# A hybrid decoder on one core: half-array products gathered into runs, and the first loads, the bias table and the first norm rearranged

## The chip, the cores and the metric

The kernel runs on 1 core of one Trainium2 chip. The metric is the device time of one execution in microseconds (us); the time before is the median of three runs. PE is TensorE, DVE is VectorE, ACT is ScalarE, POOL is GpSimd, SP is SyncE, which issues most of the transfers.

## The reference

Two layers of a decoder over 256 tokens of width 1024, all in float32. Each layer normalises `x`, projects it, runs three groups of heads, and adds the result to `x`; then a SwiGLU feed-forward part does the same.

```python
def reference(x, ...):
    for l in range(DEPTH):                       # 2
        h = rms_norm(x, attn_norm[l])
        proj = h @ w_in[l]
        r_q, r_k, r_v, r_g, n_q, n_kv, n_g, gm_z = jnp.split(proj, split_points, axis=-1)
        ret_o = retention(rope(r_q), rope(r_k), r_v, r_g)            # 6 heads of 64
        nsa_o = nsa(n_q, n_kv, n_g, ..., rel_bias)                   # 6 heads, 2 key groups
        gm_o = spatial_gating(gm_z, gm_ws[l], gm_b[l])
        x = x + jnp.concatenate([ret_o, nsa_o, gm_o], -1) @ w_out[l]
        h = rms_norm(x, ffn_norm[l])
        gate, up = jnp.split(h @ w_gate_up[l], 2, axis=-1)
        x = x + (jax.nn.silu(gate) * up) @ w_down[l]
    return x
```

Retention forms scores of queries and keys per head in chunks of 128 tokens, multiplies them by a decay and sums values with them. The sparse attention `nsa` adds a bias from a table of 32 buckets by 6 heads (`rel_bias`) that depends on the distance of query and key alone, so that each row of the bias is the row before, shifted by one.

## The kernel before

The weights, 109.86 MB in all with the other loads, stream from HBM in 102 pieces per layer (`PIECES`, L69 to L87). A piece goes into one of three staging buffers `wst`, ACT casts it to the matmul format (`whi`, six buffers), DVE subtracts the cast from the original (`wlo`, six buffers), and PE multiplies with both parts, so that each product is made of three: high by high, high by low, low by high. `stream_load`, `stream_hi` and `stream_lo` (L463 to L497) are these three steps. The normalised `x` is split in the same way into `hh` and `hl` (both in the tile `hcat`).

The projection `w_in` is cut into seven groups of columns, in the order `nk`, `nq`, `gm`, `nv`, `rq`, `rk`, `rg` (`ORDER`, L49): keys, queries, gated part, values of the sparse attention, then the four groups of retention. `nk` has 5 pieces, `nq` and `gm` 4, `nv` 3, the others 4. `project` (L1271) issues 48 products for a group: 8 slices of the inner dimension, 2 tiles of 128 tokens, 3 products. They write the PSUM banks `acc`; all else on PE writes the banks `sm`. Behind the groups come the output projection, the feed-forward part's first matrix in 11 chunks, and its second.

Nobody writes the order of instructions by hand. Each part of the work is a generator that yields operations; the class `Desk` (L259) holds a clock for each engine with cost estimates (`_cost_PE` and the like, L200) and picks at each step the waiting operation of best priority on the engine that is free first. A yielded list goes to its engine without a break. The order so found is fixed when the kernel is built; at run time an engine works its own queue in order and waits on semaphores.

What the change touches:

- `START` and `load_start` (L155, L558): the first transfers on SP. `x` comes in four quarters (two tiles of tokens, two halves of columns), "w" stands for the next piece of weights. The small table `par` (gains) stands between them. `norm_part` (L643) transposes a quarter with four products, scales it on ACT and subtracts on DVE; `norm_scale` (L676) works out the reciprocal root of one tile's mean square by some 15 operations of one column on DVE.
- `warm_up` (L546): products of zeros ("fillers", `sm<-w2k`) that PE is given while it has nothing else before the end of the first project.
- `load_layer` and `setup_bias` (L579, L600): the other small loads, and the bias. One product of the one-hot table `oh` with `relb` gives a row of 384 values for each of 6 heads on 6 partitions; a POOL transfer writes it 33 times to the DRAM tensor `scr`; four POOL transfers read it back, shifted by one for each partition, as `B` (128 partitions, 6 heads, 256 keys). POOL copies parts of it to `Bc`. `unit` (L1004) needs both for the scores of a head.
- `retention` (L1159): `scores(p)` (L1168) yields for a pair of heads a list of two products of 256 and one of two products of 128 columns, each over 64 rows of the array (`sm<-qkT`, 64*128 in the trace); then per head a list of six products of 64 columns onto half of the array's columns (`sm<-rv,S`, 128*64).
- `pv` (L1059): for each of three pairs of heads one product with `vbd` (96 rows, compressed part) and eight with `V` (`sm<-PT,V`, 128*64), which all add into one bank. `PT` holds the attention weights.

Of the kernel before, what the change touches and what calls it, by code (L numbers as in the profile page):

```python
# [9 lines left out]
F32 = mybir.dt.float32  # L10
F32R = mybir.dt.float32r
I32 = mybir.dt.int32
# [142 lines left out]
START = [(0, 0), "w", (1, 0), "w", "w", (0, 1), (1, 1), "w"]  # L155
# [28 lines left out]
class Engine:  # L184
# [5 lines left out]
    def __getattr__(self, method):  # L190
        fn = getattr(self.eng, method)

        def make(*a, prio=None, lat=True, **k):
            dur, table = getattr(self, "_cost_" + self.name)(method, a, k)
            banks = {x.tensor.name for x in (*a, *k.values()) if _psum(x)}
            return Op(self.name, lambda: fn(*a, **k), dur, table, lat, prio, banks)  # L196

        return make
# [60 lines left out]
class Desk:  # L259
# [4 lines left out]
    def __init__(self, preload):  # L264
        self.preload = preload
        self.free = {e: 0.0 for e in self.LAT}
        self.free["DMA"] = 1500.0
# [123 lines left out]
class Trunk:  # L391
    def __init__(self, ctx, tc, x, wts, cst, oh, relb, par, w1, w2, wsT, out):
# [17 lines left out]
        self.scale2 = [self.fixed(f"scale2{t}", [128, 1]) for t in range(2)]  # L410
# [15 lines left out]
        self.started = False  # L426

# [58 lines left out]
    def stream_lo(self):  # L486
        for i in range(L * len(PIECES)):
# [8 lines left out]
            self.desk.give(self.wst, self.st.pop(i))  # L496
# [23 lines left out]
    def setup(self):  # L520
# [16 lines left out]
        self.ev_cst, self.ev_bias = Event(), Event()  # L537
# [8 lines left out]
    def warm_up(self):  # L546
# [5 lines left out]
        while not self.started:  # L552
            n = 256 if self.desk.free["PE"] < Desk.COLD else 128
            yield self.PE.matmul(ps[:, :n], w[:, :128], w[:, :n], start=True, stop=True, lat=False, prio=2000)
# [3 lines left out]
    def load_start(self):  # L558

        SP, fire, lat = self.SP, self.desk.fire, self.desk.LAT["DMA"]  # L560
        yield SP.dma_start(self.ident, self.d["cst"][:, C_ID : C_ID + 128], lat=False)
        i = 0
        for step in START:
# [9 lines left out]
            if step == (0, 0):  # L573
                yield SP.dma_start(self.par, self.d["par"][0], lat=False)
                fire(self.ev_par[0], lat)
# [3 lines left out]
    def load_layer(self, l):  # L579
# [6 lines left out]
        yield SP.dma_start(self.wsT, self.d["wsT"][l].rearrange("p (g t) -> p g t", g=4))  # L586
        yield G.tensor_tensor(
            self.wsT, self.wsT, self.tri[:, None, :].to_broadcast([128, 4, 128]), op=ALU.mult
        )
# [6 lines left out]
        if l == 0:  # L596
            yield SP.dma_start(self.cst[:, C_DEC:], self.d["cst"][:, C_DEC:])
            self.desk.fire(self.ev_dec)

    def setup_bias(self):  # L600

        G, GQ, PE = self.G, self.GQ, self.PE
        oh = yield Need(self.w2k)
        ext = yield Need(self.w2k)
        rb = self.tiny("rb", [33, 6])
# [1010 lines left out]
```

## Time and profile before

| | |
|---|---|
| median of 3 runs | 645.78 us (645.46 to 646.02) |
| the profiled execution, own time | 646.46 us |
| its span, first to last instruction | 644.7 us |
| PE busy | 635.1 us |
| DVE, ACT, POOL busy | 452.9, 364.8, 11.0 us |
| mean granted clock of TensorE | 0.997 |

The profile follows one execution. The durations in it are of that execution, whose time is 1.76 us more than its span and 0.68 us above the median. Products are pipelined on PE: the length shown for one product reaches to its modelled end, so the pace is read from one row's start to the next row's start. All operations carry the line of one helper (L196), so rows are told apart by tile names: `out<-in`, buffer numbers left out. A name such as 128*64 behind MATMUL is the part of the array (rows*columns) that is used; `x16` counts passes, two for each float32 product. A bracket at the end of a row is the idle time ahead of it and what ended it. The granted clock is the share of TensorE's full clock.

### The profile page before, as it was taken

To read this page: it belongs to the slowest core of one execution; us is meant where nothing else is said; L and a number is where in the kernel's file an instruction comes from. 1 tells how busy PE (TensorE), PEld (TensorE's weight loads), DVE (VectorE), ACT (ScalarE), POOL (GpSimd) and SP (SyncE) were. 2 spreads that over 40 slices of the span, in tenths; PEclk is the share of its full clock that TensorE was granted. 3 is DMA by queue.
4 is the path that set the end of the run, shared out by engine and by line. 5 is a ranking of instruction groups with operands and counts; after the bars stand their busy time and mean duration, and the time that the engine had idled before them with its cause. 6 is when DMAs were issued, how large, how long until landed. Compare 5 with 4: busy or idle time off the path is not lost.

```text
span 644.7 us, 9955 instructions
## 1 busy us (share of the span) xinstructions
PE 635.1 (99%) x3628; PEld 533.6 (83%) x3628; DVE 452.9 (70%) x1046; ACT 364.8 (57%) x685; POOL 11.0 (2%) x28
## 2 busy tenths in 40 slices
PE   8979999999999999999999999999999999999998
PEld 7768887788888888888887888788888888888886
DVE  5867988488677677664388899865867677776441
ACT  7648963576456555543377795444755555545330
POOL 0120000000000000010000000000000000000000
PEclk9999999999999999999999999999999999999999
DMA  8885245157555565566546522534665556565631
GB/s 257 284 228 175 91 123 181 66 166 231 190 180 192 185 196 192 185 257 204 163 135 196 196 92 64 173 110 149 186 191 185 193 195 187 174 197 184 192 114 65
DMA packets 32816, 111.63 MB, mean 173 GB/s; under 512 B 4339, under 2 KB 4851, under 8 KB 32512
## 3 DMA queue, kind: packets, MB, share of 16 engines
q1 hardware_dynamic: 32256, 109.86, 52.4%
q0 software_dynamic: 512, 1.14, 0.9%
q8 instruction: 28, 0.46, 0.3%
q14 instruction: 20, 0.16, 0.1%
HBM read 109.64 MB, written 1.35 MB: 172 GB/s over the span
## 4 chain that ended last, share of the span: by engine, by line
PE 89%; DMA 5%; ACT 2%; DVE 2%; issue 1%; SPq 0%; ACTq 0%
PE acc L196 60%; PE sm L196 29%; DMA wst<-in_wts_dram 5%; ACT whi L196 1%; DVE wlo L196 1%; DMA x<-in_x_dram 1%; DVE x L196 0%; SPq L196 0%; ACT w2k L196 0%; ACT L402 0%; ACT L196 0%; DVE Kl L196 0%; ACT Kh L196 0%; ACT hcat L196 0%; ACT w1k L196 0%
## 5 line engine op out<-in xcount | busy, mean ns | idle before, releaser
L196 DVE TENSOR_TENSOR wlo<-wst,whi 128x1024 fp32r<-128x1024 f32 (+3 forms) x204 | 245.0, 1202 | 140.8 <-ACT whi L196 139.6
L196 ACT CAST whi<-wst 128x1024 fp32r<-128x1024 f32 (+3 forms) x204 | 209.2, 1028 | 195.0 <-issue 49.7
L196 PE MATMUL acc<-whi,hcat 128*128 128x512 f32 (+2 forms) x512 | 141.2, 381 | 0.0
L196 PEld LDWEIGHTS acc<-whi,hcat 128*128 128x128 f32 x512 | 91.6, 189 | 15.0 <-issue 0.7
L196 PE MATMUL acc<-hcat,whi 128*128 128x512 f32 x320 | 101.2, 396 | 0.0
L196 PE MATMUL sm<-hcat,whi 128*128 128x512 f32 x320 | 99.7, 392 | 0.0
L196 PE MATMUL acc<-wlo,hcat 128*128 128x512 f32 (+2 forms) x256 | 80.6, 381 | 0.0
L196 PEld LDWEIGHTS sm<-hcat,whi 128*128 128x128 f32 x320 | 60.0, 188 | 14.2
L196 PEld LDWEIGHTS acc<-hcat,wlo 128*128 128x128 f32 x320 | 58.8, 188 | 11.7
L196 PE MATMUL sm<-hcat,wlo 128*128 128x256 f32 x320 | 64.4, 282 | 0.0
L196 PE MATMUL acc<-hcat,wlo 128*128 128x256 f32 x320 | 64.1, 282 | 0.0
L196 PEld LDWEIGHTS acc<-wlo,hcat 128*128 128x128 f32 x256 | 46.8, 189 | 7.8 <-issue 0.3
L196 PEld LDWEIGHTS acc<-hcat,whi 128*128 128x128 f32 x320 | 50.9, 190 | 1.7
L196 PE MATMUL acc<-whi,ah 128*128 128x512 f32 (+1 forms) x176 | 50.0, 378 | 0.0
L196 PE MATMUL acc<-whi,al 128*128 128x512 f32 (+1 forms) x176 | 50.0, 378 | 0.0
L196 PE MATMUL acc<-wlo,ah 128*128 128x512 f32 (+1 forms) x176 | 49.9, 377 | 0.0
L196 PEld LDWEIGHTS sm<-hcat,wlo 128*128 128x128 f32 x320 | 49.6, 190 | 0.0
L196 PEld LDWEIGHTS acc<-whi,ah 128*128 128x128 f32 x176 | 31.9, 188 | 5.5
L196 PEld LDWEIGHTS acc<-wlo,ah 128*128 128x128 f32 x176 | 31.8, 188 | 5.5
L196 PEld LDWEIGHTS acc<-whi,al 128*128 128x128 f32 x176 | 31.8, 188 | 5.5
L196 ACT ACTIVATE hcat<-sm,par 128x128 fp32r<-128x128 f32 x64 | 18.6, 379 | 9.2 <-PE sm L196 9.2
L196 DVE SCALAR_TENSOR_TENSOR hcat<-sm,par,hcat 128x128 fp32r<-128x128 f32 x64 | 18.5, 344 | 4.5 <-ACT hcat L196 4.5
(212 smaller groups left out, 726.6 us busy)
## 6 DMA issues: line engine op xcount, KB each, us to landing
wst<-in_wts_dram SPq DMA_DIRECT2D x186, 512.0 KB, 3.8
wst<-in_wts_dram SPq DMA_DIRECT2D x8, 384.0 KB, 3.0
w<-in_w_dram SPq DMA_DIRECT2D x2, 1024.0 KB, 7.0
wst<-in_wts_dram SPq DMA_DIRECT2D x4, 411.0 KB, 4.4
x<-in_x_dram SPq DMA_DIRECT2D x4, 256.0 KB, 5.3
wst<-in_wts_dram SPq DMA_DIRECT2D x4, 256.0 KB, 3.3
cst<-in_cst_dram SPq DMA_DIRECT2D x1, 768.0 KB, 5.3
B<-scr POOLq DMA_DIRECT2D x4, 192.0 KB, 6.2
```

What stands on the lines that cost most here:

```text
L196: return Op(self.name, lambda: fn(*a, **k), dur, table, lat, prio, banks)
```

## The change

Two things are changed. In retention the products that use part of the array are put in three lists per layer: the scores of the first two pairs of heads; the scores of the third pair with the sums of heads 0 to 3; the sums of heads 4 and 5. In the attention sums the three `vbd` products come first and then all 24 `PV` products.

At the start, the quarters of `x` are loaded in another order (both tiles of the first half ahead of the weights), `par` goes out on ACT's queue, and `norm_first` treats both tiles of a half at once. `norm_scale` treats both tiles in one list of 14 operations, for all norms. `setup_bias` starts at once; its product writes each head's row to 11 partitions, 66 in all, and the copy to `scr` writes three repeats from each. The loads of `B` move from POOL's to SP's queue and stand between the loads of pieces, as do the other small loads. Four slices of `PT`, which is not needed before the attention, serve as more staging buffers for the early pieces. In `project` the product with the low part of the weights comes last of the three.

```diff
-START = [(0, 0), "w", (1, 0), "w", "w", (0, 1), (1, 1), "w"]
+START = [(0, 0), (1, 0), "w", "w", (0, 1), (1, 1), "w", "w"]
+
+NR, NREP = 33, 3
+
+EXTRA, EXTRA_UNTIL = 4, 9
...
-            self.desk.give(self.wst, self.st.pop(i))
+            st = self.st.pop(i)
+            if i < EXTRA_UNTIL or all(st is not x for x in self.extra):
+                self.desk.give(self.wst, st)
...
+        self.nc.scalar.dma_start(self.par, self.d["par"][0])
+        fire(self.ev_par[0], 3500)
...
+        w1 = lambda j: SP.dma_start(
+            self.w1[:, j], self.d["w1"][l].rearrange("p (j a e) -> p j a e", j=2, a=16)[:, j], lat=False
+        )
+        w2 = lambda: SP.dma_start(self.w2, self.d["w2"][l])
+        wsT = lambda: SP.dma_start(self.wsT, self.d["wsT"][l].rearrange("p (g t) -> p g t", g=4))
+        bias = lambda q: SP.dma_start(self.B[q : q + NR - 1], self.bias_rows(q), lat=q + NR - 1 >= 128, times=2)
...
+        yield self.loaded[5]
+        yield wsT()
+        yield causal()
         self.desk.fire(self.ev_lay[l])
-        if l == 0:
-            self.desk.fork(self.setup_bias())
-        yield SP.dma_start(self.w1, self.d["w1"][l].rearrange("p (j a e) -> p j a e", j=2, a=16), lat=False)
-        yield SP.dma_start(self.w2, self.d["w2"][l])
+        yield self.ev_scr
+        for i, q in zip((6, 8, 9, 11), range(0, 128, NR - 1)):
+            yield self.loaded[i]
+            yield bias(q)
+        self.desk.fork(self.setup_compressed_bias())
+        yield self.loaded[12]
+        yield w1(0)
+        yield self.loaded[14]
...
+        n = NR // NREP
...
+        yield G.tensor_copy(wide, rb[:, :, None].to_broadcast([33, 6, n]))
         ps = yield Need(self.sm)
-        yield PE.matmul(ps[:6, :NB], rb, oh[:33, :NB], start=True, stop=True)
-        yield self.A.copy(ext[:6, :NB], ps[:6, :NB])
+        yield PE.matmul(ps[: 6 * n, :NB], wide.rearrange("p h c -> p (h c)"), oh[:33, :NB], start=True, stop=True)
+        yield self.A.copy(ext[: 6 * n, :NB], ps[: 6 * n, :NB])
         self.desk.give(self.sm, ps)
-
-
         dpool = self.ctx.enter_context(self.tc.tile_pool(name="scr", bufs=1, space=bass.MemoryType.DRAM))
-        scr = dpool.tile([6, 33, NB], F32, name="scr")
-        yield GQ.dma_start(scr, ext[:6, None, :NB].to_broadcast([6, 33, NB]))
+        self.scr = dpool.tile([6 * n, NREP, NB], F32, name="scr")
+        yield GQ.dma_start(self.scr, ext[: 6 * n, None, :NB].to_broadcast([6 * n, NREP, NB]))
...
+    def norm_first(self, c):
+
+        gain = lambda k: self.par[:, P_G1 + k : P_G1 + k + 1]
+        lat = self.desk.LAT
+        for t in range(2):
+            yield self.ev_x[t][c]
+        for ks in ((4 * c, 4 * c + 1), (4 * c + 2, 4 * c + 3)):
+            ps = yield Need(self.sm)
+            p4 = ps.rearrange("p (k t n) -> p k t n", k=2, t=2)
+            yield [
+                self.transpose(p4[:, j, t], self.x[t][:, k * 128 : k * 128 + 128])
+                for j, k in enumerate(ks)
+                for t in range(2)
+            ]
+            yield self.ev_par[0]
...
+            for j, k in enumerate(ks):
+                yield self.A.activation(self.hh[:, k, :], flat[:, j], AF.Copy, scale=gain(k), lat=False)
+                self.desk.fire(split[j], lat["ACT"])
...
+        ax, y, z, i = (self.tiny("nr_" + n, [128, 2], I32 if n == "i" else F32) for n in "ayzi")
+        mult, add = ALU.mult, ALU.add
+        ops = [
+            V.tensor_tensor(ax, self.sums[:, :, 0], self.sums[:, :, 1], op=add),
+            V.tensor_scalar(ax, ax, 1.0 / D, EPS, op0=mult, op1=add),
+            V.tensor_single_scalar(i, ax.bitcast(I32), 1, op=ALU.logical_shift_right),
+            V.tensor_scalar(y.bitcast(I32), i, -1.0, float(0x5F3759DF), op0=mult, op1=add),
+        ]
+        for n in range(3):
+            ops += [
+                V.scalar_tensor_tensor(z, y, -0.5, y, op0=mult, op1=mult),
+                V.tensor_tensor(z, z, ax, op=mult),
+                V.scalar_tensor_tensor(self.rstd2 if n == 2 else y, z, 1.5, y, op0=add, op1=mult),
+            ]
+        ops.append(V.tensor_scalar_mul(self.axe2, ax, EPS))
+        for op in ops:
+            op.dur = self.desk.LAT["DVE"]
+        yield ops
...
+        pos = []
+        for j in range(3):
+            po = yield Need(self.sm)
+            pos.append(po)
         ops = [
             mm(
-                po[:, :256], self.vbd[:, 2 * j : 2 * j + 2, :].rearrange("p g d -> p (g d)"), self.pcT,
-                start=True, stop=False,
+                pos[j][:, :256], self.vbd[:, 2 * j : 2 * j + 2, :].rearrange("p g d -> p (g d)"), self.pcT,
+                start=True, stop=False, lat=False,
             )
+            for j in range(3)
         ]
-        for b in range(2):
-            for kt in range(2):
-                qs = slice(128 * kt, 256)
-                ks = slice(0, 256) if kt == 0 else slice(256, 384)
-                for g in range(2):
-                    vs = slice(b * 128 + g * 64, b * 128 + g * 64 + 64)
-                    ops.append(
-                        mm(
-                            po[64 * g : 64 * g + 64, qs], self.Vt[kt][:, vs], self.PT[:, 6 * b + 3 * g + j, ks],
-                            start=False, stop=b == 1 and kt == 1,
+        yield ops
...
+        for j in range(3):
+            ops = []
+            for b in range(2):
+                for kt in range(2):
+                    qs = slice(128 * kt, 256)
+                    ks = slice(0, 256) if kt == 0 else slice(256, 384)
+                    for g in range(2):
+                        vs = slice(b * 128 + g * 64, b * 128 + g * 64 + 64)
+                        ops.append(
+                            mm(
+                                pos[j][64 * g : 64 * g + 64, qs], self.Vt[kt][:, vs],
+                                self.PT[:, 6 * b + 3 * g + j, ks],
+                                start=False, stop=b == 1 and kt == 1, lat=False, prio=-2,
+                            )
                         )
-                    )
-        yield ops
-        yield from self.split(self.nsh[j], self.nsl[j], po[:, :256])
-        self.desk.give(self.sm, po)
-        self.desk.fire(self.ev_ns[j])
+            yield ops
+            self.desk.fire(done[j], self.desk.LAT["PE"])
...
+        first = yield from open_pair(0)
+        second = yield from open_pair(1)
+        yield scores(first) + scores(second)
+        self.desk.fork(decay(0, first))
+        self.desk.fork(decay(1, second))
+        for h in range(4):
+            yield done[h]
...
+        yield scores(third) + list(sums(range(4)))
...
+        self.desk.fork(decay(2, third))
+        for h in (4, 5):
             yield done[h]
-            if h == 0:
-                for t in range(2):
-                    p = yield Need(self.sm)
-                    po.append(p)
-            hs = slice(h * 64, h * 64 + 64)
-            a = at[h]
-            yield [
-                PE.matmul(
-                    po[q][r : r + 64, hs], a[:, c + r : c + r + 64], self.rv[k][:, hs], start=k == 0, stop=k == q
-                )
-                for q, k, c in ((0, 0, 0), (1, 0, 128), (1, 1, 256))
-                for r in (0, 64)
-            ]
-            give(self.S, a)
+        yield list(sums((4, 5)))
...
-            for n_th, (x, w) in enumerate(((self.hh, wh), (self.hh, wl), (self.hl, wh))):
...
+            wh, products = self.part(self.hi, i, a), [(self.hh, "hi"), (self.hl, "hi"), (self.hh, "lo")]
+            for n_th, (x, half) in enumerate(products):
+                if apart and n_th:
+                    for ev in x_wait[1] if n_th == 1 else [self.ready[i]]:
+                        yield ev
+                w = wh if half == "hi" else self.part(self.lo, i, a)
...
+        for c in range(2):
+            fork(self.norm_first(c), 2)
+        fork(self.norm_scale(), 4)
+        fork(self.setup_bias(), 3)
...
+            if l == 0:
+                flat = self.PT.rearrange("p u n -> p (u n)")
+                self.extra = [flat[:, i * 1024 : i * 1024 + 1024] for i in range(EXTRA)]
+                for st in self.extra:
+                    self.desk.give(self.wst, st)
```

Where the order of instructions moves, three places:

SP, layer 0, the loads from the twelfth piece of weights on (`wst`, and in the change also `PT`, are staging buffers of weights; `cst` the constants; `w` the weights of the compressed part). Before:

```order
L196 DMA wst_75<-in_wts_dram 128x1024
L196 DMA cst<-in_cst_dram 128x1536
L196 DMA wst_73<-in_wts_dram 128x1024
L196 DMA wst_74<-in_wts_dram 128x822
L196 DMA wst_75<-in_wts_dram 128x822
L196 DMA wst_73<-in_wts_dram 128x548
```

and with the change, from the ninth piece on:

```order
L201 DMA wst_72<-in_wts_dram 128x1024
L201 DMA wst_73<-in_wts_dram 128x1024
L201 DMA PT_133<-in_wts_dram 128x1024
L201 DMA B<-scr 32x6x256 x3
L201 DMA PT_133<-in_wts_dram 128x1024 x2
L201 DMA PT_133<-in_wts_dram 128x822
L201 DMA B<-scr 32x6x256
L201 DMA wst_71<-in_wts_dram 128x822
```

Three loads of `B`, which were on POOL's queue, now stand in SP's behind the eleventh piece and ahead of the twelfth.

PE, retention of layer 0, where sums and scores alternate (`acc` are products of the group `rk` or `rg`, `S` the decayed scores). Before:

```order
L196 MATMUL acc_63<-wlo_84,hcat 128x384
L196 MATMUL sm_70<-rv_0_136,S_0_144 64x64 x2
L196 MATMUL sm_68<-rv_0_136,S_0_144 64x64 x2
L196 MATMUL sm_68<-rv_0_137,S_0_144 64x64 x2
L196 MATMUL acc_64<-wlo_84,hcat 128x384
L196 MATMUL acc_63<-whi_78,hcat 128x384
L196 MATMUL sm_70<-rv_0_136,S_0_143 64x64 x2
L196 MATMUL sm_68<-rv_0_136,S_0_143 64x64 x2
L196 MATMUL sm_68<-rv_0_137,S_0_143 64x64 x2
L196 MATMUL acc_64<-whi_78,hcat 128x384
L196 MATMUL acc_63<-whi_79,hcat 128x384
L196 MATMUL sm_70<-rv_0_136,S_0_145 64x64 x2
```

and with the change, the start of the list that begins with the third pair's scores:

```order
L201 MATMUL acc_64<-whi_76,hcat 128x384
L201 MATMUL sm_68<-qkT_138 128x256
L201 MATMUL sm_70<-qkT_138 128x256
L201 MATMUL sm_68<-qkT_138 128x128
L201 MATMUL sm_70<-qkT_138 128x128
L201 MATMUL sm_67<-rv_0_136,S_0_142 64x64 x2
L201 MATMUL sm_69<-rv_0_136,S_0_142 64x64 x2
L201 MATMUL sm_69<-rv_0_137,S_0_142 64x64 x2
```

Scores and sums now follow one another with no `acc` product between.

PE, the attention sums of layer 0. Before:

```order
L196 MATMUL sm_68<-pcT_135,vbd_134 128x256
L196 MATMUL sm_68<-PT_133,V_0_131 64x256 x2
L196 MATMUL sm_68<-PT_133,V_0_132 64x128 x2
L196 MATMUL sm_68<-PT_133,V_0_131 64x256 x2
L196 MATMUL sm_68<-PT_133,V_0_132 64x128 x2
L196 MATMUL sm_67<-pcT_135,vbd_134 128x256
L196 MATMUL sm_67<-PT_133,V_0_131 64x256 x2
L196 MATMUL sm_67<-PT_133,V_0_132 64x128 x2
```

and with the change:

```order
L201 MATMUL acc_64<-whi_74,hcat 128x384
L201 MATMUL sm_70<-pcT_135,vbd_134 128x256
L201 MATMUL sm_69<-pcT_135,vbd_134 128x256
L201 MATMUL sm_67<-pcT_135,vbd_134 128x256
L201 MATMUL sm_70<-PT_133,V_0_131 64x256 x2
L201 MATMUL sm_70<-PT_133,V_0_132 64x128 x2
L201 MATMUL sm_70<-PT_133,V_0_131 64x256 x2
L201 MATMUL sm_70<-PT_133,V_0_132 64x128 x2
```

The three `vbd` products stand in a row, and the `PV` products of all three pairs behind them.

## Rows read from the trace of the kernel before

**Rows 1.** The page, part 1: busy us (share) xinstructions of each engine.
```profile
PE 635.1 (99%) x3628; PEld 533.6 (83%) x3628; DVE 452.9 (70%) x1046; ACT 364.8 (57%) x685; POOL 11.0 (2%) x28
```

**Rows 2.** Windows: length; busy us (xcount) of PE, PEld, DVE, ACT, POOL; PEclk; DMA share; GB/s.
```profile
45.00:50.00 5.00, 2.81 (x10) 2.52 (x11) 4.51 (x10) 2.77 (x5) 1.33 (x3) 0.71 1.01 202
50.00:55.00 5.00, 5.00 (x38) 4.80 (x37) 2.76 (x5) 2.70 (x5) 1.50 (x10) 0.95 0.91 283
70.00:75.00 5.00, 5.00 (x25) 4.16 (x24) 5.00 (x27) 4.87 (x15) 0.00 (x0) 1.00 0.31 102
```

**Rows 3.** Chain that ended last, 0 to 60 us: start us, us, what.
```profile
2.58 4.57 DMA x<-in_x_dram
...
15.81 9.12 PE acc L196 x40
...
35.38 9.14 DMA wst<-in_wts_dram
...
46.50 7.09 DMA wst<-in_wts_dram
```

**Rows 4.** Timeline of POOL: start us, us, operation xcount, [idle before <- releaser].
```profile
33.09 0.74 POOL L196 DMA_DIRECT2D scr<-w2k  x1 [12.64 <-ACT w2k L196]
43.80 2.27 POOL L196 DMA_DIRECT2D B<-scr  x4 [9.97 <-DMA scr<-w2k]
```

**Rows 5.** Timeline of DVE, around 45 us, and the decay of two heads in retention.
```profile
45.46 1.02 DVE L196 TENSOR_TENSOR wlo<-wst,whi 128x822 fp32r<-128x822 f32 x1 [5.70 <-ACT whi L196]
...
109.83 1.15 DVE L196 TENSOR_TENSOR S<-sm,cst 128x256 f32<-128x256 f32 x4
```

**Rows 6.** Timeline of PE, 43 to 51 us.
```profile
47.20 1.54 PE L196 MATMUL sm<-cst,w2k 128*128 128x128 f32 x6 [3.48 <-DVE w2k L196]
...
49.39 1.05 PE L196 MATMUL acc<-wlo,hcat 128*128 128x512 f32 x2
50.24 1.03 PE L196 MATMUL acc<-whi,hcat 128*128 128x512 f32 x4
```

**Rows 7.** Timeline of PE, first products and first unit of the sparse attention.
```profile
7.61 0.47 PE L196 MATMUL acc<-whi,hcat 128*128 128x512 f32 x1
...
8.15 0.61 PE L196 MATMUL sm<-w2k 128*128 128x128 f32 x4
...
57.99 0.50 PE L196 MATMUL sm<-Kh,Q 128*128 128x512 f32 x1 [0.24 <-DVE Kl L196]
```

**Rows 8.** Timeline of PE, retention of layer 0.
```profile
106.92 0.62 PE L196 MATMUL acc<-whi,hcat 128*128 128x384 f32 x2
107.46 0.49 PE L196 MATMUL sm<-qkT 64*128 64x128 f32 x4
...
111.49 0.57 PE L196 MATMUL sm<-rv,S 128*64 128x64 f32 x12
111.99 0.45 PE L196 MATMUL acc<-wlo,hcat 128*128 128x384 f32 x1
...
114.08 0.70 PE L196 MATMUL sm<-qkT 64*128 64x256 f32 x4
114.72 0.57 PE L196 MATMUL sm<-rv,S 128*64 128x64 f32 x12
```

**Rows 9.** Timeline of PE, retention of layer 1.
```profile
417.41 0.93 PE L196 MATMUL sm<-qkT 64*128 64x128 f32 x8
418.27 0.62 PE L196 MATMUL acc<-wlo,hcat 128*128 128x384 f32 x2
```

**Rows 10.** Timeline of PE, attention sums of layer 0.
```profile
99.19 1.52 PE L196 MATMUL sm<-PT,V 128*64 128x256 f32 x16
100.64 0.70 PE L196 MATMUL sm<-pcT,vbd 96*128 96x256 f32 x2
101.27 1.52 PE L196 MATMUL sm<-PT,V 128*64 128x256 f32 x16
```

**Rows 11.** Groups of DVE by form: operation xcount | busy us, mean ns | idle before.
```profile
L196 DVE COPY rstd<-nr_y 128x1 f32<-128x1 f32 x8 | 1.2, 150 | 0.1
```

More of the change, by code (lines that the diff above doesn't have):

```diff
@@ L409, in __init__ @@
         self.sm = Pool([bank(f"sm{i}") for i in range(4)])
-        self.scale2 = [self.fixed(f"scale2{t}", [128, 1]) for t in range(2)]
+        self.norms = 0
         self.wst = Pool([self.fixed(f"wst{i}", [128, 1024]) for i in range(3)])
@@ L605, in setup_bias @@
         rb = self.tiny("rb", [33, 6])
+        wide = self.tiny("rbw", [33, 6, n])
         yield GQ.dma_start(oh[:33, :NB], self.d["oh"])
@@ L639, in norm_state @@
         self.ss = [[Event(), Event()] for _ in range(2)]
-        self.rstd = [self.tiny(f"rstd{t}", [128, 1]) for t in range(2)]
-        self.axe = [self.tiny(f"axe{t}", [128, 1]) for t in range(2)]
+        self.norms += 1
+        self.rstd2 = self.tiny(f"rstd{self.norms}", [128, 2])
+        self.rstd = [self.rstd2[:, t : t + 1] for t in range(2)]
+        self.axe2 = self.tiny("axe", [128, 2])
+        self.axe = [self.axe2[:, t : t + 1] for t in range(2)]
+        self.sums = self.tiny("ss", [128, 2, 2])
     def norm_part(self, t, c, gcol, nb=4):
@@ L1087, in pv, with finish @@
-        yield ops
-        yield from self.split(self.nsh[j], self.nsl[j], po[:, :256])
-        self.desk.give(self.sm, po)
-        self.desk.fire(self.ev_ns[j])
+        yield ops
+        done = [Event() for _ in range(3)]
+        def finish(j):
+            yield done[j]
+            yield from self.split(self.nsh[j], self.nsl[j], pos[j][:, :256])
+            self.desk.give(self.sm, pos[j])
+            self.desk.fire(self.ev_ns[j])
+        for j in range(3):
+            self.desk.fork(finish(j))
@@ L1174, in scores, with decay @@
                 heads.append((a, ps, self.qkT[r : r + 64, 3 + p, :], self.qkT[r : r + 64, p, :]))
-            yield [PE.matmul(ps[:, :256], kT[:, :128], qT, start=True, stop=True) for _, ps, kT, qT in heads]
-            yield [
+            return heads
+        def scores(heads):
+            return [PE.matmul(ps[:, :256], kT[:, :128], qT, start=True, stop=True) for _, ps, kT, qT in heads] + [
                 PE.matmul(ps[:, 256:384], kT[:, 128:], qT[:, 128:], start=True, stop=True) for _, ps, kT, qT in heads
             ]
+        def decay(p, heads):
             for h, (a, ps, _, _) in zip((2 * p, 2 * p + 1), heads):
@@ L1312, in both @@
                 self.done(i)
-        if apart:
+        if apart == "first":
+            for k, (i, a) in enumerate(ks):
+                yield from both(k, i, a)
+        elif apart:
             end = Event(), Event()
@@ L1521, in main @@
                 if l == 0 and i == 0:
-                    fork(self.load_layer(0), 401)
-                yield from self.project(idx("in", name), _width(name), i == 0, then)
+                    fork(self.load_layer(0), 399)
+                yield from self.project(idx("in", name), _width(name), i == 0 and ("again" if l else "first"), then)
             def mixed(k, t):
```

160 lines of the change are left out of this document (102 added, 58 removed).

## The prediction

> **What bounds the kernel now.** I read the page's busy times first: PE is busy for 635.1 us, 99% of the span, and no other engine passes 70% [rows 1]. So time can only come from PE's queue: from products that are slower than they need be, or from PE standing still. The chain of waits gives the price of an undisturbed product: forty products of 512 columns in 9.12 us, 0.228 us each [rows 3]; by columns one of 384 should take 0.171 us. The windows then show where PE is not at that pace. There is one such place in the front part: in 45 to 50 us it is busy for 2.81 us of 5, at a granted clock of 0.71, and 0.95 in the next 5 us [rows 2]. Behind 60 us it is busy nearly without a break, also where VectorE is busy for all of 5 us [rows 2].
>
> The stall. PE waits 3.48 us for VectorE's `w2k` (the normalised queries) before the transposes at 47.20 [rows 6]. VectorE was idle itself for 5.70 us, with its queue held by the subtraction for a piece of weights [rows 5]; that piece took 9.14 us from its issue at 35.38 to its landing, and a later one 7.09 us [rows 3]. In the same stretch the copy `scr<-w2k` is under way: issued at 33.09, and POOL waits 9.97 us for it before it issues the four loads of `B` at 43.80 [rows 4]. Behind the stall the products come 0.85 us for two (49.39 to 50.24), 0.425 each [rows 6]: TensorE is at 1.2 GHz, the lower of its two levels, after standing still, and back at 2.4 GHz soon after.
>
> The half-array products. Two full-array products of 384 columns that stand between two lists of scores take 0.54 us (106.92 to 107.46) where 0.34 is due: 0.20 us for going in and out [rows 8]. Inside a list there is a second price. A list of two scores products of 256 columns, two passes each, takes 0.64 us (114.08 to 114.72) [rows 8]. Layer 1 has a list where the scheduler happened to put two products of 128 and two of 256 columns in a row: 0.86 us (417.41 to 418.27) [rows 9]. With a fixed price a and c per column, a + 512c = 0.64 and a + 768c = 0.86 give c = 0.00086 and a = 0.20 us: paid once per list, not once per product. A list of six sums, twelve passes of 64 columns on half the array each, takes 0.50 us (111.49 to 111.99) [rows 8]; at half of c per pass that is 0.33 us of work and 0.17 us of fixed price.
>
> **The change part by part.**
>
> 1. *Retention gathered.* Layer 0 leaves the full array nine times, with six lists of scores and six of sums: 9 x 0.20 + 6 x 0.20 + 6 x 0.17 = 4.0 us. The change leaves it three times: scores of two pairs; scores of the third pair with the sums of four heads; the last two sums. That is 3 x 0.20 + 2 x 0.20 + 2 x 0.17 = 1.3 us, so 2.7 us are saved; I take 2.6, as two of the old lists stand beside transposes, which pay less. Layer 1 now has seven excursions with five lists of scores and six of sums: 1.4 + 1.0 + 1.0 = 3.4 us, so 2.1 are saved.
>
> 2. *Attention sums gathered.* Per layer three times one `vbd` product and eight `PV` products: 1.45 us for the eight (99.19 to 100.64), 0.63 for the `vbd` product (to 101.27) [rows 10]. Two of three returns go; each takes the fixed price of a `vbd` list (like scores, 0.20) and of a `PV` list (same tile as the sums, 0.17) with it: 0.74 us per layer. In sum 2.6 + 2.1 + 1.4 = 6.1 us. The lower bound is 2.0: only the ten saved excursions' 0.20 on the full-array side.
>
> 3. *The stall at 43.5 to 51 us.* The bias table is now worked out at the start, and its copy leaves from 66 partitions in place of 6. POOL can issue it when the bias product (in the first project) has been copied out by ScalarE, at about 16 us. If it takes as long as before (33.09 to 43.80, 10.7 us [rows 4]) it lands at 27; with no time at all at 16. I take 22, the bytes being as many and the source eleven times as wide. SP's queue now holds the first three `B` loads behind the eleventh piece of weights and before the twelfth to fourteenth, so these wait for it. PE needs the twelfth (third of the gated group's four) after the first project, four pieces (48 products) and half of the next 48: 22 + 72 x 0.228 + some 3 us of transposes = 41 us. A load took 9.14 us at worst [rows 3], the cast and the subtraction some 2 us: it must be issued by 30, so 22 to 27 is hidden. The four more staging buffers let the fourth to seventh and the eleventh to fourteenth piece be fetched ahead of the casts. So the idle 3.48 us go, and the slow stretch with them: six transposes and four products took 3.04 us (47.20 to 50.24) [rows 6] where 6 x 0.1 + 4 x 0.228 = 1.5 are due; 1.6 us with the rest. The short wait before the first unit at 57.99 (0.24) [rows 7] goes too, since `B` is there long before. Sum: 5.3 us, and what is late next is the first project.
>
> The DMA page's rule bears on it, with no effect on the sum. The Trainium skill, "DMA: Bandwidth & Descriptors", section "Why a DMA increments its semaphore by 16 and not by 1", says that a transfer uses the largest number of engines up to 16 that divides the slowest dimension of both sides: 6 for the old copy, 11 for the new. By it the 10.7 us would be some 5.8, an estimate; no run here shows the new copy.
>
> 4. *The first project.* The first product is at 7.61 now, 0.46 us behind the fifth load, which took 4.57 us from 2.58 [rows 3, 7]. In the change the first weights are the fourth load, with as many bytes in front as that fifth one had, so they land at about 7.1; then ScalarE casts them and only after that scales the first transposes, 1.1 us: first product at 8.3, 0.7 later (bounds 0 and 1.5). Four transposes move behind it (4 x 0.1 = 0.4). Of the fillers behind it, 12 are now 5: at 0.09 each (four from 8.15 in 0.36) [rows 7] 0.6 less. The bias product moves from the second project into the first and costs the same. Net 0.5 us later.
>
> 5. *Norms and the rest.* One chain of 14 small operations on VectorE replaces two interleaved ones; at 0.15 us each [rows 11] 2.1 us in which nothing else runs there. At the start it stands ahead of the subtraction for the seventh piece, which PE needs some 3 us later; at the three other norms PE has 27 products (6.2 us) of the next group in front of what needs it. In retention the decay of two heads takes 1.15 us [rows 5], 2.3 for four, and sixteen products and a third pair of scores (3.4 us) stand between on PE. Cover is there, but thinner, and between 60 and 85 us VectorE has no idle time [rows 2] while PE reaches the attention sums 14 products earlier. Bounds 0 and 3 us; I take 0.5. Moving `par` to ScalarE's queue, the split load of `w1`, and the order of products in a piece change nothing that PE waits for.
>
> Sum: -6.1 - 5.3 + 0.5 + 0.5 = -10.4. The profiled execution took 646.46 us (span 644.7 and 1.76 around it) and becomes 636.1; it lies 0.68 above the median of the runs shown, 645.78, from which the same sum gives **635.4 us**. A difference under about 1.3 us (0.2%) can't be told from none here.
>
> **Rivals.**
>
> *The start gives less* (chance 0.17). The stall at 43.5 us is replaced by smaller ones: at the start ScalarE's cast and VectorE's 14 operations stand in line before what PE wants, and PE, which has fewer fillers, stands still ahead of its first product. For it: VectorE's queue in order is what held PE at 47 us [rows 5, 6]. Against it: the supply is 7 buffers deep. If PE starts at the lower clock, eight products cost 8 x 0.2 = 1.6 us more, and one held piece as much again: 635.4 + 3.2 = 638.6. The Trainium skill, "TensorE: Matmul & The Clock Gate", section "What's actually happening", says that the throttled clock is the default and activity releases it; the 0.71 in rows 2 behind the idle 3.48 us agrees, and it speaks against taking fillers away.
>
> *The price inside the lists belongs to each product* (0.07). Then gathering saves only the full-array side, 2.0 of 6.1 us: 639.5. Against it stands the list of four in rows 9, which would have taken 1.06.
>
> *Both fall together* (0.03): the wait for weights stays and the lists wait for decays: 645.
>
> *Slower: SP held by `B`* (0.03). SP issues in order, and three loads of `B` wait for the copy with the twelfth piece behind them. It decides when the copy lands after 30 us; from there each us costs PE one. If POOL got to the copy no earlier than now and it landed at 43.8 [rows 4], the twelfth piece would be there at about 54, and PE would idle for 13 us and run slow for 1.6 more: 635.4 + 14.6 = 650. For it: the same copy held up a queue in the trace. Against it: every input of the copy is at hand 15 us earlier.
>
> **How the numbers follow.** My forecast has 0.70: from 633.2 (no new wait and a first product no later, 1.2 us, and some 30 removed prices read to 0.03, 1.0) to 638 (2.6 of the 3 us of new waits). Adding the first two rivals, up to 639.8, leaves out under 2 in 10. Faster by more than 0.2% holds for the forecast and the first two rivals: 0.94. Within 0.2%: 0.03. Slower: 0.03.
>
> **What would show it.** The granted clock of 45 to 50 us is 1.00 and PE's wait for `w2k` is gone. The copy to `scr` lands before 28 us. The first group of the rotary queries begins at about 52.5 us (57.4 now). A list of eight scores products takes about 1.5 us, the 24 `PV` products some 4.0. It is wrong if PE shows a new wait of over 1 us ahead of the attention sums or in retention, or if the second project begins after 24 us.

## The result and the profile after

| | before | after |
|---|---|---|
| median, range | 645.9 us (645.46 to 646.32), 4 runs | 637.94 us (637.33 to 639.74), 4 runs |
| ratio, 95% interval | | 0.9881 (0.9861 to 0.9902) |
| profiled execution, span | 646.46, 644.7 us | 638.01, 636.2 us |
| PE busy | 635.1 us | 630.5 us |
| mean granted clock | 0.997 | 1.000 |

The kernel is faster by 8.0 us; 10.4 were forecast. The median lies 0.06 us inside the upper end of the range, 638.

The windows of the kernel after, over the first two stretches of [rows 2] (for each engine busy time and instructions, then the granted clock, the share of the DMA engines and GB/s):

```profile
45.00:50.00 5.00, 5.00 (x37) 4.77 (x36) 4.84 (x7) 4.87 (x7) 0.00 (x0) 1.00 0.73 261
50.00:55.00 5.00, 5.00 (x40) 4.86 (x39) 3.97 (x17) 4.98 (x9) 0.00 (x0) 1.00 0.37 135
```

PE is busy for all of 45 to 50 us, and the granted clock is 1.00 where it was 0.71. All waits of PE in the whole execution, and below them SP's in 14 to 32 us (total, times, longest):

```profile
PE sm L201 <- DVE w2k L201: 1.4, 1, 1.4
PE sm L201 <- DMA x<-in_x_dram: 0.5, 1, 0.5
PE acc L201 <- ACT hcat L201: 0.3, 1, 0.3
PE sm L201 <- DVE amx L201: 0.2, 1, 0.2
...
SPq L201 <- DMA scr<-w2k: 6.5, 1, 6.5
```

The 1.4 us stand ahead of the first filler, in both kernels (before, PE waits for `w2k` twice, 4.9 us in all). Of the 3.48 us of [rows 6] nothing is left. SP waits 6.5 us for the copy, as the slower rival had it, but PE does not notice: the pieces ahead of the three `B` loads carry it. The copy and the loads behind it, on POOL and SP (start, length, in brackets the idle time and what ended it):

```profile
15.28 0.76 POOL L201 DMA_DIRECT2D scr<-w2k  x1 [7.87 <-ACT w2k L201]
...
22.27 1.30 SPq L201 DMA_DIRECT2D B<-scr  x3
```

POOL issues the copy at 15.28 and SP is released at 22.27: 7.0 us where the one from 6 partitions took 10.7 [rows 4]. The estimate by the rule of the Trainium skill, "DMA: Bandwidth & Descriptors", section "Why a DMA increments its semaphore by 16 and not by 1", was 5.8: the direction is right, and the measured gain, 3.7 us, is three quarters of the rule's 4.9.

PE's timeline of the kernel after: the first product, the start of the rotary queries, the gathered attention sums, the two lists of scores and the sums.

```profile
8.34 0.72 PE L201 MATMUL acc<-whi,hcat 128*128 128x512 f32 x2 [0.34 <-ACT hcat L201]
...
52.78 0.40 PE L201 MATMUL acc<-whi,hcat 128*128 128x512 f32 x1
...
92.27 1.46 PE L201 MATMUL sm<-pcT,vbd 96*128 96x256 f32 x6
93.66 4.12 PE L201 MATMUL sm<-PT,V 128*64 128x256 f32 x48
97.71 1.09 PE L201 MATMUL sm<-cst,w1k 128*128 128x128 f32 x8
...
100.51 1.58 PE L201 MATMUL sm<-qkT 64*128 64x256 f32 x16
102.02 0.97 PE L201 MATMUL acc<-whi,hcat 128*128 128x384 f32 x4
...
105.02 0.92 PE L201 MATMUL sm<-qkT 64*128 64x256 f32 x8
105.87 1.62 PE L201 MATMUL sm<-rv,S 128*64 128x64 f32 x48
107.42 0.62 PE L201 MATMUL acc<-wlo,hcat 128*128 128x384 f32 x2
```

From start to start: eight scores products (sixteen passes) take 1.51 us, the 24 `PV` products 4.05, the sums of four heads 1.55. The short lists of [rows 8 to 10] are gone.

Where the gain stands and where some of it is lost, by the starts of products in PE's two timelines:

| product | before | after | saved so far | in this stretch |
|---|---|---|---|---|
| first | 7.61 | 8.34 | -0.73 | -0.73 |
| first of the rotary queries | 57.36 | 52.78 | 4.58 | 5.31 |
| first with `rth` (output projection, layer 0) | 133.40 | 125.67 | 7.73 | 3.15 |
| first of layer 1 | 328.60 | 322.71 | 5.89 | **-1.84** |
| first of layer 1's feed-forward part | 455.28 | 446.49 | 8.79 | 2.90 |
| last | 641.25 | 632.68 | 8.57 | -0.22 |

Two of these products as the timeline has them, before and then after:

```profile
133.40 0.39 PE L196 MATMUL acc<-whi,rth 128*128 128x512 f32 x1
...
328.60 0.62 PE L196 MATMUL acc<-whi,hcat 128*128 128x512 f32 x2
```

```profile
125.67 0.40 PE L201 MATMUL acc<-whi,rth 128*128 128x512 f32 x1
...
322.71 0.62 PE L201 MATMUL acc<-whi,hcat 128*128 128x512 f32 x2
```

The start gives 4.6 us, the stretches with the attention of the two layers 3.15 and 2.90. But between the output projection of layer 0 and layer 1, a part that the change doesn't mention, 1.84 us go. The chain of waits has there one unbroken row, the second feed-forward matrix of layer 0 (start, length, count), first of the kernel before, then of the one after:

```profile
267.48 52.82 PE acc L196 x233
```

```profile
259.96 54.37 PE acc L201 x233
```

The same 233 products of 512 columns take 0.2267 us each before and 0.2333 after, at a clock of 1.00 in both, with no wait in either. One difference between the two programs is where the tiles lie in SBUF; that it is the cause has to be shown. The change drops the two `scale2` tiles and makes other small tiles of other sizes, and everything that is allocated behind them moves. In the built programs the operands of the residual products (`gmh`, `ah` and their like, which the output projection and the second feed-forward matrix multiply with the weights) begin at byte 150208 of a partition before, 64 x 2347, and at 150304 after, 32 more than a multiple of 64.

### The profile page after: what moved, and what is told of

Same layout as the page of the kernel before. It is cut to its first block, busy times and chain, and to the rows that moved or that the text cites. A ratio compares the mean times of both kernels' runs of the same rounds, so it can differ in the third digit from the quotient of the medians.

```text
span 636.2 us, 9911 instructions
## 1 busy us (share of the span) xinstructions
PE 630.5 (99%) x3638; PEld 534.7 (84%) x3638; DVE 448.5 (70%) x970; ACT 365.8 (57%) x679; POOL 10.7 (2%) x25
## 4 chain that ended last, share of the span: by engine, by line
PE 98%; DMA 1%; DVE 0%; SPq 0%; issue 0%; ACT 0%
PE acc L201 69%; PE sm L201 29%; DMA wst<-in_wts_dram 1%; SPq L201 0%; DVE S L201 0%; DVE x L201 0%; ACT hcat L201 0%; DVE amx L201 0%; ACT whi L201 0%
## 5 line engine op out<-in xcount | busy, mean ns | idle before, releaser
L201 DVE TENSOR_TENSOR wlo<-wst,whi 128x1024 fp32r<-128x1024 f32 (+3 forms) x196 | 234.0, 1197 | 131.6 <-ACT whi L201 130.6
L201 ACT CAST whi<-wst 128x1024 fp32r<-128x1024 f32 (+3 forms) x196 | 200.7, 1028 | 183.7 <-PE sm L201 49.6
L201 PE MATMUL acc<-whi,hcat 128*128 128x512 f32 (+2 forms) x512 | 139.4, 379 | 0.3 <-ACT hcat L201 0.3
L201 ACT ACTIVATE hcat<-sm,par 128x128 fp32r<-128x128 f32 (+1 forms) x56 | 17.3, 393 | 10.1 <-PE sm L201 9.8
L201 DVE SCALAR_TENSOR_TENSOR hcat<-sm,par,hcat 128x128 fp32r<-128x128 f32 (+1 forms) x56 | 17.4, 362 | 6.0 <-ACT hcat L201 6.0
```

## The experiments

All times are medians, each beside runs of the kernel before on the same chip, which gave 646.80 (experiments 1 to 4), 646.89 (5, 6, 7 and 10) and 645.91 us (8, 9, 11 and 12). Between chips the ratios are the better measure.

**1, 2. The address alone: after_pad and before_pad.** The theory: 32 bytes of address are the missing 2 us. One unused tile of 32 bytes behind the small ones moves the operands of the kernel after onto a multiple of 64, and those of the kernel before off it.

```diff
             k.desk.run(k.main())
+            k.V.memset(k.tiny("pad", [128, 8]), 0.0).call()
```

> The changed kernel with one more unused tile of 32 bytes per partition behind the small tiles, so that the tiles which only the output projection and the feed-forward part's second matrix use as stationary operands (gmh to rtl, ah, al) begin at a multiple of 64 bytes again, as in the kernel before, and not 32 behind one. Theory (address): products of 512 columns in the two residual parts of layer 0 go back from 0.2333 to 0.2267 us, 96 x 0.0067 + 264 x 0.0067 = 2.4 us, and some 0.4 to 0.6 in layer 1; the time falls by 2.4 to 3.2 us, to about 635.2. Rival (a phase that sets in by chance or by the new order of instructions): the pace of these stretches stays at 0.233 and the time within 0.5 us of 637.9.

> The kernel before with the same 32 unused bytes, so that the same tiles lie 32 bytes behind a multiple of 64. Theory (address): the residual products of layer 0 slow from 0.2267 to 0.2333 us and the time rises by 2.4 to 3.2 us, to about 648.6. Rival (a phase, or the new order): no change beyond 0.5 us.

after_pad: 634.64 us, ratio 0.9818 (0.9799 to 0.9837). before_pad: 649.17 us, ratio 1.0040 (1.0025 to 1.0054). The same row of the chain, of after_pad and of before_pad:

```profile
259.09 53.34 PE acc L201 x233
```

```profile
267.90 54.36 PE acc L196 x233
```

The pace moves with the address in both kernels, with the rest of the program unchanged: 0.2333 us off the multiple of 64 in both, on it 0.2289 in the kernel after and 0.2267 in the kernel before. So after_pad does not come back to the 0.2267 that was expected. The change as it is loses about 3.3 us to its address (637.94 against 634.64; 3.2 from the first product to the last in the two traces), and the kernel before loses 2.4 when given the same misplacement. So this part is shown.

**3, 4. One half of the change each: before_gather and after_nogather.** The first is the kernel before with `retention` and `pv` of the change; the second is after_pad with those of the kernel before. The core of the first (the second is its reverse):

```diff
-            yield [PE.matmul(ps[:, :256], kT[:, :128], qT, start=True, stop=True) for _, ps, kT, qT in heads]
-            yield [
+            return [PE.matmul(ps[:, :256], kT[:, :128], qT, start=True, stop=True) for _, ps, kT, qT in heads] + [
                 PE.matmul(ps[:, 256:384], kT[:, 128:], qT[:, 128:], start=True, stop=True) for _, ps, kT, qT in heads
             ]
...
+        yield scores(first) + scores(second)
...
+        yield scores(third) + list(sums(range(4)))
...
+        yield list(sums((4, 5)))
```

> The kernel before with the gathered retention and attention sums alone; start, bias, norms and addresses as before. Theory (a fixed price per list): 645.9 - 6.1 = 639.8, with half-array lists as long as in the changed kernel's trace (eight scores products 1.5 us, 24 PV products 4.05 us), and 0 to 0.5 us of new waits. Rival (price per product): 2.0 us less, 643.9.

> The changed kernel with retention and attention sums as before, and with the 32 bytes that put the residual operands at a multiple of 64. Theory (the two halves of the change add up, the address being a third, separate term): the start alone, 4.6 us at the beginning of the rotary queries, less up to 0.5 of later waits: 645.9 - 4.3 = 641.6. Rival (the start's gain is used up behind, where VectorE has no idle time): 643 or more.

before_gather: 640.29 us, ratio 0.9900 (0.9884 to 0.9916), 6.5 us saved. By starts of products it has 3.06 us of its gain at `rth` and 2.92 more across layer 1's attention. after_nogather: 640.02 us, ratio 0.9895 (0.9879 to 0.9910), 6.8 us saved where 4.3 were expected; 5.25 of it is there at the start of the rotary queries, 5.23 still at layer 1's `rth`, and of the rest 0.94 comes in layer 1's second feed-forward matrix. There the address acts again: the products of 512 columns take 0.2317 us each in the kernel before (mean from start to start) and 0.2282 in the two with the small tile. So the start is worth about 5.3 us by itself. Gathering is worth 6.5 us alone and 5.4 on top of the changed start (640.02 less the 634.64 of after_pad).

**5. The early copy alone: before_early_bias.** The kernel before, with `setup_bias` begun at the start and nothing else: 6 partitions, three staging buffers, the loads of `B` on POOL.

```diff
-        if l == 0:
-            self.desk.fork(self.setup_bias())
...
             fork(self.norm_scale(t), 4)
+        fork(self.setup_bias(), 3)
```

> The kernel before with one edit: the setup of the bias is started with the first norm and no longer behind the load of wsT. Its copy still leaves from 6 partitions, B is still loaded by POOL, three staging buffers, start and norms as before. Theory (the stall at 43.5 us is the slow copy and the loads of B, falling on the pieces of the gated and value groups): with the copy at about 16 us the stall goes and with it 3.5 + 1.6 us; 645.9 - 4.5 = 641.4. Rival (three staging buffers and the other small loads hold the pieces up): a wait of over 2 us stays between 35 and 50 us and the time is 644 or more.

655.27 us, ratio 1.0128 (1.0111 to 1.0144): 8.4 us slower than the kernel before. The theory is out. The rival's two signs are there, though it did not say that the time would rise. PE's longest waits; the pieces of weights in the chain; the windows in which PE stands still:

```profile
PE sm L196 <- DVE w1k L196: 6.6, 1, 6.6
PE acc L196 <- ACT whi L196: 2.6, 2, 2.4
...
15.28 9.73 DMA wst<-in_wts_dram
...
27.37 11.20 DMA wst<-in_wts_dram
...
40.00:45.00 5.00, 0.00 (x0) 0.00 (x0) 4.10 (x12) 4.34 (x10) 0.99 (x1) 0.62 0.68 233
45.00:50.00 5.00, 4.27 (x12) 3.52 (x13) 4.87 (x16) 3.25 (x8) 0.00 (x0) 0.50 0.45 138
```

The copy leaves at 14.62 and lands at about 25; the piece issued beside it takes 9.73 us, and the one beside the loads of `B` 11.20. That is the collision of the kernel before [rows 3, 4], moved to a place where PE has less work in front of it. Being early is not what cures the stall; by itself it costs.

**6, 7, 8. What does cure it: no_extra, scr6, scr6_no_extra.** From after_pad: without the four more staging buffers; with the copy from 6 partitions again; with both. (The unused tile is sized in each so that the residual operands stay where they are in after_pad.)

```diff
-NR, NREP = 33, 3
+NR, NREP = 33, 33
...
-EXTRA, EXTRA_UNTIL = 4, 9
+EXTRA, EXTRA_UNTIL = 0, 9
```

> The changed kernel with aligned operands (after_pad) without the four more staging buffers in PT. Theory (the buffers only bridge the time in which SP waits for the copy, and PE is that far behind): within 0.7 us of after_pad. Rival (they carry the start): SP is held at B with only three pieces ahead, PE waits between 25 and 45 us, 2 us or more slower than after_pad.

> after_pad with the copy to scr from 6 partitions (33 repeats each) as in the kernel before; the residual operands at the same addresses as in after_pad. Theory: the copy takes about 10.7 us instead of 7.0 from its issue, lands at about 26, SP's queue stands until then, and PE notices nothing: within 0.4 us of after_pad. Rival (the faster copy is what removes the stall): 1 us or more slower.

> after_pad with both protections taken away: the copy to scr from 6 partitions, and no staging buffers in PT; B still in SP's queue behind the copy, small loads between the pieces. Theory (either protection is enough, both together carry the start): loads that are issued while the slow copy is under way take 9 us or so, only three are in flight, and PE waits for 2 to 6 us between 25 and 45 us: 637 to 641. Rival (neither matters, SP's order alone is what helped): within 1 us of no_extra, 636.5 at most.

no_extra: 635.46 us (635.38 to 635.71), ratio 0.9820 (0.9807 to 0.9833), not to be told from after_pad on its other chip (0.9818), with new waits of PE of 0.6 and 0.2 us. scr6: 634.00 us (633.46 to 634.82), ratio 0.9798 (0.9783 to 0.9812), not to be told from after_pad, though its copy takes 11.3 us. scr6_no_extra: 641.20 us (639.98 to 641.96), ratio 0.9921 (0.9903 to 0.9938), 6.6 us more than after_pad. Its wait, the piece in its chain, and two windows:

```profile
PE sm L201 <- ACT w1k L201: 3.8, 1, 3.8
...
17.55 9.76 DMA wst<-in_wts_dram
...
25.00:30.00 5.00, 1.20 (x7) 0.66 (x6) 2.27 (x4) 2.66 (x9) 1.56 (x2) 0.96 0.79 212
30.00:35.00 5.00, 5.00 (x18) 3.97 (x17) 3.74 (x10) 4.97 (x10) 0.00 (x0) 0.69 0.88 226
```

PE stands idle for 3.8 of 5 us, and the granted clock falls to 0.69 behind it: the stall of the kernel before is back, some 18 us earlier. So the wide source and the buffers each do nearly the whole work, and only the loss of both shows.

The two kernels without the buffers differ in the width of the copy alone. The pieces of weights and the copy in 14 to 21 us, first no_extra (66 partitions), then scr6_no_extra (6; count, KB each, median us from issue to landing):

```profile
wst<-in_wts_dram SPq DMA_DIRECT2D x3, 512.0 KB, 5.9
scr<-w2k POOLq DMA_DIRECT2D x1, 297.0 KB, 6.5
```

```profile
wst<-in_wts_dram SPq DMA_DIRECT2D x3, 512.0 KB, 9.2
scr<-w2k POOLq DMA_DIRECT2D x1, 297.0 KB, 10.8
```

With the same bytes from fewer partitions the copy takes longer, and so do the pieces beside it.

**9. The queue of the `B` loads: b_pool.** after_pad with these loads back on POOL's queue, so that SP's queue does not wait for the copy.

```diff
-        bias = lambda q: SP.dma_start(self.B[q : q + NR - 1], self.bias_rows(q), lat=q + NR - 1 >= 128, times=2)
+        bias = lambda q: self.GQ.dma_start(self.B[q : q + NR - 1], self.bias_rows(q), lat=q + NR - 1 >= 128)
```

> after_pad with the four loads of B back on POOL's queue, all issued when the copy has landed, beside the pieces on SP's queue. Theory (seven buffers carry the pieces over the collision): within 0.7 us of after_pad, although the pieces issued beside B take longer. Rival (B in SP's order is what keeps the pieces on time): PE waits again, 1.5 us or more slower.

635.07 us (634.67 to 636.71), ratio 0.9834 (0.9814 to 0.9855): no difference from after_pad that can be told. SP's 6.5 us of waiting cost nothing here.

**10. Another address: pad352.** The kernel after, with a tile of 352 bytes in place of 32; the operands then lie at 128 beyond a multiple of 512, as `whi` does.

```diff
+            k.V.memset(k.tiny("pad", [128, 88]), 0.0).call()
```

> The changed kernel with 352 unused bytes, so that the residual operands have the same place as the weight buffers whi modulo 512 bytes, as in the kernel before (192 and 192 there). after_pad has them at a multiple of 64, 192 bytes from that place, and runs at 0.2291 us a product where the kernel before has 0.2267. Theory (the offset of the two operands counts, beyond 64 bytes): 0.2267 in layer 0, 0.6 us for 264 + 96 products at least, 1.0 with layer 1; about 633.7. Rival (a multiple of 64 is all there is): the pace and the time of after_pad, 634.6.

634.67 us, ratio 0.9808 (0.9794 to 0.9822), the time of after_pad. The row of the chain:

```profile
259.03 52.82 PE acc L201 x233
```

Layer 0's second matrix is back at 0.2267 us, the pace of the kernel before. But layer 1's second matrix, at 0.2282 in after_pad, now runs at 0.2317, so the sum stays. Both are the paces of the kernel before. So the theory holds for the pace, though not for the time. All traces but the profiled one of first_earlier (see the end) fall into three classes, by the place of the operand `ah` and of `whi` in the built programs (pace in us; layer 0 by the chain's row, layer 1 as mean from start to start):

| place of `ah` | traces | layer 0 | layer 1 |
|---|---|---|---|
| that of `whi` modulo 512 | before, before_gather, before_early_bias, pad352 | 0.2267 | 0.2317 |
| 192 bytes on from it | after_pad and six of its variants | 0.2289 | 0.2282 |
| 32 bytes off a multiple of 64 | after, before_pad | 0.2333 | 0.2331 to 0.2333 |

Why the first two classes change places between the layers is left open, and no other distance was run.

**11, 12. Two tries at a faster version: first_earlier and gu_runs.** first_earlier is after_pad with another landing time for the first piece in the planner, so that ACT scales the first transposes ahead of its first cast. gu_runs adds to it the products of a piece of the first feed-forward matrix in runs of eight of 512 and eight of 256 columns, in place of four and four, for fewer changes of shape.

```diff
-            self.desk.fire(self.loaded[i], self.desk.LAT["DMA"])
+            self.desk.fire(self.loaded[i], self.desk.LAT["DMA"] + (300 if i == 0 else 0))
...
-                for op in low + wide if last else wide + low:
-                    yield op
+                wides += wide
+                lows += low
+            for op in lows + wides if last else wides + lows:
+                yield op
```

> after_pad with the planner told that the first piece of weights arrives 0.3 us later, which puts the scaling of the first transposes ahead of the first cast on ScalarE and leaves no fillers behind the first product. Theory (the cast, the scaling and the fillers are in line before and behind the first product, as the first project's end, 1.6 us later than before, says): the second project begins 0.4 to 0.9 us earlier and so the end, about 634.0. Rival (the landing of the loads sets the first project): within 0.3 us of after_pad.

> first_earlier with the first feed-forward matrix in runs of eight products of 512 and eight of 256 columns instead of four and four. In all traces the pace behind a change of shape is 0.231 to 0.237 us for four to eight products and then 0.227; in these groups of four it is 0.2326 throughout. Theory (the slower pace belongs to the first products behind a change): three or four of eight at 0.227, 640 products of 512 columns in all, 1 to 2 us off. Rival (it belongs to operands or banks): no change beyond 0.4 us.

first_earlier: 633.56 us (median of six, of which one is told of at the end), ratio 0.9814 (0.9792 to 0.9837). gu_runs: 634.70 us (633.19 to 635.55), ratio 0.9820 (0.9799 to 0.9842). By their times neither can be told from after_pad. In gu_runs one group became cheaper, first after_pad, then gu_runs (busy time, mean ns):

```profile
L201 PE MATMUL acc<-hcat,whi 128*128 128x512 f32 x320 | 101.2, 396 | 0.0
```

```profile
L201 PE MATMUL acc<-hcat,whi 128*128 128x512 f32 x320 | 100.1, 393 | 0.0
```

From its first product to that of the second matrix, the first feed-forward matrix takes 123.87 and 123.88 us in the two layers of gu_runs and 124.42 in both of after_pad: the longer runs are worth 1.1 us in these traces, the lower end of what was expected. The profiled execution of gu_runs gave that back at the start, where `x` landed late and the first product stood at 9.64. After_pad, scr6, pad352, first_earlier and gu_runs lie between 633.6 and 634.7 us, ahead of both kernels; which of them is fastest is not shown.

## Why the prediction was right in sign and 2.4 us too large

*The stall (5.3 forecast).* Right in mechanism. The wait and the slow clock are gone, and the copy landed at 22.3 where 22 was taken. From the second project to the rotary queries 6.6 us are saved; about 0.75 of that is the bias product, which left this stretch, so 5.9 stand against 5.3. What the text left unsaid is that its three reasons are not of one kind: the early issue harms by itself (experiment 5), while faster copy and deeper buffers are each nearly enough (6 to 8).

*The first project (0.5 lost).* Too small by some 0.75 us. The first product came at 8.34, as worked out (8.3). The second project began at 22.73, before the 24 that would have spoken against the text, but 2.04 later than before, where 0.5 and the bias product's 0.8 make 1.3. The 0.6 us that fewer fillers were to give did not come: ten of their passes, 0.94 us in all, stand behind the first product in both traces, and the transposes there cost 0.6 more, not 0.4. This error and that of the stall have opposite signs, so that the start as a whole, 4.58 us against 4.8, looks better forecast than it was.

*Gathering (6.1).* Right in mechanism, and near in size. The fixed price belongs to the list, not to the product: eight scores products take 1.51 us (forecast 1.5), the 24 `PV` products 4.05 (4.0). Gathering is worth 6.5 us alone and 5.4 beside the changed start (experiments 3 and 4). That the two attention parts of the table add up to 6.05 is partly chance: after_nogather, without gathering, saves 0.62 and 0.61 in these two stretches, and the kernel after has 0.55 less there than after_pad (3.50 and 3.10), from which only the address separates it. The first rival, a start that gives less, and the second, a price per product, are out: the second would have left 2.0 of the 6.1. By the number alone the first rival (638.6) lies nearer to 637.94 than the forecast does; the waits that it needs are not in the trace.

*New waits (0.5).* PE shows a single new one between the rotary queries and the end, 0.2 us for `amx` (a small tile of the sparse attention). In the table it doesn't show as a loss; the 0.62 and 0.61 of after_nogather say that the rest of the change gains a little there. Of these, 0.24 can be the wait at 57.99 [rows 7] that the stall's sum had counted; where the rest comes from is open.

*The slower rival.* Its mechanism is there: SP stood 6.5 us behind the copy. Its price is nothing, because the copy landed well ahead of 30 us, the point from which it was to decide; with the loads off SP's queue the time is the same (experiment 9).

*The step that failed* is the price of a product. The text took 0.228 us for 512 columns from one row [rows 3] and used it as a constant, and its sum has no term for the place of the operands. The new norms and the new setup of the bias drop some small tiles and size others anew. Part 5 does not name this; it changed no wait, but it moved every operand allocated behind them, and with that the pace of 654 residual products of 512 columns: 1.84 and 0.22 us in the table, 2.4 to 3.3 by experiments 1 and 2. That is about the size of the missing 2.4 us; the errors of the other terms nearly cancel. The price is a constant only while the tiles stay where they are. That the median still lies inside the range is luck: the upper end, 638, was there for 2.6 us of new waits on PE, which did not come.

## What to carry to other kernels

When a change adds, drops or resizes a small tile, compare the addresses of the large operands before and after it, and set them right with an unused tile; then time the change. Price a mode of the array per list, from two lists of different length, and gather lists where buffers allow. A stall that has several remedies should be tested with each taken away alone and together: one that seems needless alone may be the other's cover.

## What was not expected of the hardware

The pace of full-array products of 512 columns depends on the address of their operands in SBUF: 0.2267 to 0.2333 us, at a clock of 1.00 and with no wait, by 32 bytes. Transfers from few partitions slow others beside them: three pieces of weights took 9.2 us (median) beside the copy from 6 partitions and 5.9 beside the one from 66, in kernels that differ in this alone; one took 11.2 beside the four loads of `B`. And one execution of first_earlier, the profiled one, took 3559 us, with only TensorE slow: its busy time rose from 630.5 us in the kernel after to 3552.6, VectorE's was 456.7 against 448.5. Products of 512 columns followed one another at 1.28 us (median) in place of 0.23. Its page has no row of the granted clock, which all other pages here have, so what the clock did is not shown. What caused it is open.
